# One encoder block: two projections at 512 columns through DRAM, and three joints' loads moved

## The chip, the cores and the metric

The kernel runs on one core of a Trainium2 chip. Its engines each work through a queue of their own in order: TensorE (PE in the profile; PEld is its weight load), VectorE (DVE), ScalarE (ACT), GpSimd (POOL) and SyncE (SP), which here only issues DMAs. The metric is the device time of one execution in microseconds (us), lower is better. Three runs of the kernel before took 1698.77 to 1700.16 us, median 1699.96.

## The reference

One layer of a hybrid encoder on 1024 tokens of 1024 channels, all in float32. Three token mixers share one input projection; then comes a gated feed-forward net.

```python
        h = _rmsnorm(x, norm_mix_g[l])
        z = h @ w_in[l].astype(jnp.float32)
        (hq, hf, hi, hg, fq, fk, fv, ff, mq, gate_logits) = jnp.split(z, pts, axis=-1)
        y_a = _hgrn2_mixer(hq, hf, hi, hg, lower_bounds[l], hgrn_norm_g[l])
        y_b = _fox_mixer(fq, fk, fv, ff, fox_f_bias[l], fox_q_norm_g[l], fox_k_norm_g[l])
...
        y_c = _memory_mixer(mq, mem_kv, mem_q_norm_g[l], mem_k_norm_g[l])
        gates = jax.nn.sigmoid(gate_logits).reshape(B, T, N_BRANCH, D_MODEL)
        merged = (gates[:, :, 0] * (y_a @ w_br_hgrn[l].astype(jnp.float32))
                  + gates[:, :, 1] * (y_b @ w_br_fox[l].astype(jnp.float32))
                  + gates[:, :, 2] * (y_c @ w_br_mem[l].astype(jnp.float32)))
        x = x + (merged @ w_out[l].astype(jnp.float32)).astype(x.dtype)
        h2 = _rmsnorm(x, norm_ffn_g[l])
        x = x + _conv_glu_ffn(h2, ffn_w_up[l], ffn_conv_w[l], ffn_conv_b[l], ffn_w_down[l]).astype(x.dtype)
```

There are 4 recurrence heads with a 128x128 state, 8 attention heads of 64 channels, and 4 heads over 256 memory tokens. The middle mixer is causal softmax attention whose logits carry a cumulated log of forget gates. Its queries and keys (`fq`, `fk`) are normalized per head. The recurrence needs values (`hi`), queries, a forget gate and an output gate.

## The kernel before

**Products.** Each float32 product is three matmuls: operands are split into a rounded part (`h`) and the rest (`l`), and `mm3` (L160 to L162) forms h·h, h·l and l·h. A `split` (L172) is a cast on ScalarE (L166) and a subtraction on VectorE (L174). Weights come by DMA into `raw` (two buffers), and their parts lie in `wh` and `wl` with three buffers each of 128x1056.

**Order.** The program is written in Python generators. `weave` (L97) interleaves them by fixed step counts, `ahead` (L148) gives attention a higher priority, `tc.issue_after` ties an instruction behind another, and a list scheduler of the framework then fixes each engine's order when the kernel is built. On the chip each engine follows its order, so an instruction that must wait holds all behind it.

**Stages.** From the start to 205 us: normalized input `u`, first gates, and pairs of 128-column chunks by a Strassen-like scheme. Then `token_major` (L704) forms projections with tokens on the partitions: for 8 blocks of 128 tokens, 8 pieces of channels and three matmuls each, 256 columns wide. It makes the attention's values `Vf` (`fox_values`), then for each pair of heads `p` its 128 key and 128 query columns (`fox_proj`, L844). A block is evicted by ScalarE into `z` (two tiles of four blocks); after four blocks the tile is normalized. `fox_prep` (L866) transposes `z` and makes the operands `kh`, `kl`, `qa`.

**Attention.** `fox_attn` (L901) takes a head in eight blocks of 128 queries, two by two. Per block: logits on TensorE into `lg` (L924, L925), bias, maximum and mask on VectorE (L930), exp on ScalarE (L940), reciprocal on VectorE (L941), scaling on GpSimd (L942). Per two blocks: transposes on TensorE into `tr` (L953 to L956), split by ScalarE and VectorE into `ph`, `pl`, and products with the head's values `vhl` into `po` (L965, L966). `vhl` is split from `Vf` by `fox_vsplit` (L896), has two buffers, and so waits for the last product two heads back. There are two `lg`, two `tr`, one `po` and three `pp` accumulators.

Between the attention's matmuls the kernel weaves others that depend on little: while head 2p runs, the projection for the next two heads; while head 2p+1 runs, three chunks of gates (`gates_early` with `NFOX`, L31). During heads 6 and 7 come the recurrence's values (`hgrn_values`, L1012), in two passes of 256 columns, whose evictions overwrite `Vf`.

**Later joints.** The branch products (`branch`, L1280) take the attention's and the recurrence's outputs, then the memory branch's, `yc`, which POOL loads in eight transfers of 512 KB (L1311). After `w_out`, `first_products` (L1425) starts the feed-forward net's first unit with operands loaded early; `second_norm` (L1413) sums squares by matmuls with `ones`, GpSimd takes the power (L179), and `spread` (L361) copies the result over partitions by matmuls (L366). `unit` (L1452) loads a unit's weights on POOL's queue (L1457). Between units of the first pair `families` splits operand blocks; two of B21's subtractions run on GpSimd.

Of the kernel before, what the change touches and what calls it, by code (L numbers as in the profile page):

```python
# [30 lines left out]
NFOX = [0, 3, 0, 3, 0, 3, 1]  # L31
# [3 lines left out]
assert 2 + NCOVER + NPAIR + sum(NFOX) == len(ORDER) and len(_dense) % 2 == 0  # L35
# [5 lines left out]
FOX_LATE = 0.2  # L41
SEQ = ("w0 x0 s0 w1 x1 s1 w2 x2 s2 w3 x3 s3 w4 x4 s4 x5 s5 x6 s6 x7 s7 u0 u1 u2 u3 mn u4 u5 u6 u7 lk k0 k1 k2 k3 lx "
# [67 lines left out]
def tile_block(ctx: ExitStack, tc: tile.TileContext, xT, memT, x_rows, mem_rows, vec, fbias, mats, hmask, w_first, w_cm, w_hi, w_fqk, w_fv,  # L110
# [77 lines left out]
    def weights(src, shape, raw=None, hl=None, parts=1):  # L188
# [4 lines left out]
        if hl is None:  # L193
            hl = [wp.tile([P, 4 * 264], F32R, tag=t, name=t, bufs=3) for t in ("wh", "wl")]
# [227 lines left out]
    def first_weights(k):  # L422
        k0, k1 = WFIRST[k]
        if k % 4 == 0:
            gw[k // 4] = [wp.tile([P, 4 * 264], F32R, tag=t, name=t, bufs=3) for t in ("wh", "wl")]
        sl = slice((k0 % 4) * 256, (k1 - 1) % 4 * 256 + 256)
        split(S, gw[k // 4][0][:, sl], gw[k // 4][1][:, sl], wg[k // 4][:, sl])
# [131 lines left out]
    class Dense:  # L559
# [16 lines left out]
        def operand(self, src):  # L576
            if self.half is None:
                self.half = [wp.tile([P, 4 * 264], F32R, tag=t, name=t, bufs=3) for t in ("wh", "wl")]
# [125 lines left out]
    def token_major(src, ncol, evac):  # L704

        with tc.issue_after(late["load"].ins):
            w = [weights(src[q], (4, ncol)) for q in range(2)]
        for tb in range(8):
            ps = ps_proj()[:, :ncol]
            tsl = slice(tb * P, (tb + 1) * P)  # L710
            for k in range(KC):
                wh, wl = w[k // 4]
                mm3(ps, uh[k][:, tsl], ul[k][:, tsl], wh[:, k % 4, :], wl[:, k % 4, :], k == 0, k == KC - 1)
# [129 lines left out]

    def fox_proj(p):  # L844

        fox_z[p] = [None, None]

        def evac(tb, ps):
            n, b = tb // 4, tb % 4
            if b == 0:  # L850
                fox_z[p][n] = pq.tile([P, 4, 256], F32, tag="z", name=f"z{p}_{n}", bufs=2)
            z = fox_z[p][n]
            S.activation(z[:, b, :], ps, AF.Copy, scale=rt[:, tb:tb + 1])
            if b == 3:
                zz = z.rearrange("p b (h d) -> p (b h) d", d=64)
                sq = pools["pf"].tile([P, 16, 64], F32, tag="pt", name="fsq", bufs=4) if p else \
                    pm.tile([P, 16, 64], F32, tag="fsq", name="fsq")
                r = cp.tile([P, 16], F32, tag="fr", name="fr", bufs=2)
                S.activation(sq, zz, AF.Square)
                V.reduce_sum(r, sq, axis=AX.X)  # L860
                rstd_small(r, r, 64)
                V.tensor_mul(zz, zz, r.unsqueeze(2).to_broadcast([P, 16, 64]))

        yield from token_major(w_fqk[p], 256, evac)

# [414 lines left out]
    def branch(br, yh, yl, js=range(8)):  # L1280
        for j in js:
            i = order.index((br, j))
            gts = []
            for n in range(2):
                gt = gate_tile()
                SP.dma_start(gt, gd[i, n])
                gts.append(gt)
            for n, ps in br_chunk(br, j, yh, yl):
# [17 lines left out]
    py = Rounded(tc, name="py", bufs=1, side="right", reuse_waits="tile")  # L1306
    yc = [[py.tile([P, T], F32R, tag=f"yc{p}{c}", name=f"yc{p}{c}") for c in range(4)] for p in "hl"]
    for c in range(4):
# [506 lines left out]
```

## Time and profile before

| what | value |
| --- | --- |
| median of three runs | 1699.96 us |
| profiled execution, its own time | 1700.23 us |
| its span | 1698.4 us |
| instructions | 24291 |
| HBM read, written | 180.72 MB, 67.93 MB |
| attention (first to last logits) | 326.7 to some 654 us |

The profile is one execution. "Busy" is the time in which an engine had an instruction at work, and its share is of the span. A group line gives line, engine, operation, output and inputs, count, then busy time in us and the mean of one in ns, then the engine's idle time just before, with what ended it. A window line gives the stretch, its length, then for PE, PEld, DVE, ACT and POOL the busy us with the number of instructions, the granted clock of TensorE, and the DMA share and GB/s.

### The profile page before, as it was taken

How to read it: one execution, taken by the hardware profiler on the slowest of the kernel's cores; microseconds unless marked ns; L12 is line 12 of the kernel's file. 1: busy time of each engine (PE TensorE's matmuls, PEld its weight loads, DVE VectorE, ACT ScalarE, POOL GpSimd, SP SyncE). 2: the span in 40 equal slices, each digit the busy share in tenths (PEclk: the TensorE clock that was granted, in tenths of full speed). 3: DMA queues.
4: the chain of work that ended last, by engine and by line, in shares of the span. 5: the costliest groups of instructions: out<-in, count | busy, mean ns of one | idle time of the engine just before them, and what ended most of it. 6: DMA issues, size and time to landing. Idle time of an engine off the chain costs nothing.

```text
span 1698.4 us, 24291 instructions
## 1 busy us (share of the span) xinstructions
PE 1691.0 (100%) x8957; PEld 1452.4 (86%) x8957; DVE 1150.8 (68%) x2057; ACT 800.9 (47%) x1428; POOL 324.6 (19%) x420
## 2 busy tenths in 40 slices
PE   9999999999999999999999999999999999999999
PEld 7888899989898998888888888888888888888887
DVE  6966455666666664886856845987878888775654
ACT  6734455545454553775631333644434444533432
POOL 0200032543433331544310000311111111100000
PEclk9999999999999999999999999999999999999999
DMA  9443232221212111110346542566544344494772
GB/s 367 157 161 106 88 139 68 77 92 51 94 59 77 63 46 57 67 32 13 106 127 209 167 186 100 165 174 169 158 139 138 118 149 143 172 363 145 251 269 87
DMA packets 83062, 227.16 MB, mean 134 GB/s; under 512 B 9712, under 2 KB 12408, under 8 KB 82816
## 3 DMA queue, kind: packets, MB, share of 16 engines
q1 hardware_dynamic: 64320, 160.54, 26.8%
q0 software_dynamic: 18048, 64.50, 13.2%
q8 instruction: 70, 1.15, 0.3%
q10 hardware_dynamic: 576, 0.59, 0.1%
q14 instruction: 48, 0.39, 0.1%
HBM read 180.72 MB, written 67.93 MB: 146 GB/s over the span
## 4 chain that ended last, share of the span: by engine, by line
PE 99%; DVE 0%; ACT 0%; DMA 0%; issue 0%; ACTq 0%; DVEq 0%
PE pp L160 21%; PE pp L162 21%; PE pp L161 21%; PE lg L160 4%; PE lg L162 4%; PE lg L161 4%; PE tr L162 3%; PE tr L161 3%; PE tr L160 3%; PE po L966 1%; PE lg L925 1%; PE lg L924 1%; PE po L965 1%; PE po L160 1%; PE po L161 1%; PE po L162 1%
## 5 line engine op out<-in xcount | busy, mean ns | idle before, releaser
L160 PE MATMUL pp<-uh,wh 128*128 128x512 f32 x412 | 163.3, 396 | 0.0
L161 PE MATMUL pp<-ul,wh 128*128 128x512 f32 x412 | 162.9, 395 | 0.0
L162 PE MATMUL pp<-uh,wl 128*128 128x512 f32 x412 | 162.5, 394 | 0.0
L161 PE MATMUL pp<-wl,uh 128*128 128x256 f32 (+1 forms) x512 | 146.3, 286 | 0.0
L162 PE MATMUL pp<-wh,ul 128*128 128x256 f32 (+1 forms) x512 | 146.1, 286 | 0.0
L160 PE MATMUL pp<-wh,uh 128*128 128x256 f32 (+1 forms) x512 | 145.6, 286 | 0.0
L166 ACT CAST wh<-s 128x512 fp32r<-128x512 f32 x110 | 66.5, 621 | 131.6 <-PE pp L161 55.1
L166 ACT CAST wh<-raw 128x1024 fp32r<-128x1024 f32 (+2 forms) x76 | 67.6, 890 | 100.6 <-PE pp L161 86.2
L166 ACT CAST wh<-rw 128x512 fp32r<-128x512 f32 x87 | 53.2, 619 | 108.1 <-PE pp L161 70.2
L160 PEld LDWEIGHTS pp<-wh,uh 128*128 128x128 f32 x512 | 97.3, 190 | 1.2
L161 PEld LDWEIGHTS pp<-wl,uh 128*128 128x128 f32 x512 | 97.4, 190 | 1.0
L162 PEld LDWEIGHTS pp<-wh,ul 128*128 128x128 f32 x512 | 97.4, 190 | 0.9
L1457 POOL DMA_DIRECT2D rw<-in_w_up x44 | 24.1, 555 | 372.4 <-DVE wl L1350 171.3
L166 ACT CAST dwh<-wr 128x1024 fp32r<-128x1024 f32 (+1 forms) x41 | 40.2, 980 | 115.8 <-PE tr L161 40.0
L162 PEld LDWEIGHTS pp<-uh,wl 128*128 128x128 f32 x412 | 77.5, 188 | 15.1
L174 DVE TENSOR_TENSOR wl<-raw,wh 128x1024 fp32r<-128x1024 f32 (+2 forms) x75 | 78.0, 1040 | 17.8 <-ACT wh L166 17.6
L160 PEld LDWEIGHTS pp<-uh,wh 128*128 128x128 f32 x412 | 77.5, 188 | 14.6
L161 PEld LDWEIGHTS pp<-ul,wh 128*128 128x128 f32 x412 | 77.5, 188 | 14.5
L940 ACT ACTIVATE pt<-pt,st 128x128 f32<-128x128 f32 (+3 forms) x64 | 49.7, 777 | 41.7 <-DVE st L937 33.9
L174 DVE TENSOR_TENSOR dwl<-wr,dwh 128x1024 fp32r<-128x1024 f32 (+1 forms) x41 | 46.3, 1129 | 31.7 <-ACT dwh L166 31.7
L942 POOL TENSOR_SCALAR pt<-pt,st 128x128 f32<-128x128 f32 (+3 forms) x64 | 49.1, 767 | 78.4 <-DVE st L941 64.1
L1350 DVE TENSOR_TENSOR wl<-rw,wh 128x512 fp32r<-128x512 f32 x69 | 47.7, 704 | 22.7 <-PE pp L162 18.2
(500 smaller groups left out, 5123.2 us busy)
## 6 DMA issues: line engine op xcount, KB each, us to landing
rw<-in_w_up POOLq DMA_DIRECT2D x44, 512.0 KB, 4.7
sd<-in_w_dn POOLq DMA_DIRECT2D x30, 512.0 KB, 6.0
br<-yd SPq DMA_DIRECT2D x30, 512.0 KB, 5.0
raw<-in_w_cm SPq DMA_DIRECT2D x24, 512.0 KB, 3.4
gd<-gt SPq DMA_DIRECT2D x48, 256.0 KB, 2.0
gt<-gd SPq DMA_DIRECT2D x48, 256.0 KB, 2.7
yd<-fc SPq DMA_DIRECT2D x44, 256.0 KB, 2.2
wr<-sd SPq DMA_DIRECT2D x20, 512.0 KB, 4.5
```

The source lines that it names most:

```text
L160: PE.matmul(ps, lh, rh, start=first, stop=False, skip_group_check=more)
L161: PE.matmul(ps, lh, rl, start=False, stop=False, skip_group_check=more)
L162: return PE.matmul(ps, ll, rh, start=False, stop=last, skip_group_check=more)
L166: return S.copy(out, in_)
L174: return (sub or V).tensor_sub(l, src, h.bitcast(F32))
L924: PE.matmul(ps[:, :w], qa[i][:, tsl], kh[i][:, s0:s0 + w], start=True, stop=False)
L925: fox_sets[p][3] = PE.matmul(ps[:, :w], qa[i][:, tsl], kl[i][:, s0:s0 + w], start=False, stop=True)
L940: S.activation(pt[:, :ns], pt[:, :ns], AF.Exp, bias=st[:, 2:3], accum_out=st[:, 3:4])
L942: G.tensor_scalar(pt[:, :ns], pt[:, :ns], st[:, 3:4], 0.0, ALU.mult, ALU.add)
L965: PE.matmul(o, vhl[:, sb, :], ph[:, src], start=(sb == 0), stop=False)
L1350: late["split"] = V.tensor_sub(l, src, h.bitcast(F32))
L1457: late["raw"] = G.dma_start(raw[:, 2 * i:2 * i + 2, :], src[:, 2 * i:2 * i + 2, :])
```

## The change

It has four parts.

1. The key and query columns of heads 4 to 7 are projected together, 512 columns at once, and so are the recurrence's 512 value columns; weights come in four pieces of two channel blocks. `wh` and `wl` get a fourth buffer, and the scratch for DMA descriptors is cut to 4096. The projection of heads 4 to 7 goes block by block to DRAM (`zd`), and `fox_load` brings two `z` tiles back per pair of heads, a head earlier than they were formed before.
2. The gates that cover the attention are dealt out anew: three, two, three and one chunks beside heads 3, 4, 5 and 6, one beside head 1.
3. The memory branch's loads are spread over the steps of the branch before it, by marks on GpSimd.
4. The second feed-forward unit's load is tied behind GpSimd's B21 subtraction.

```diff
-NFOX = [0, 3, 0, 3, 0, 3, 1]
+NFOX = 10
...
+WIDE = 4
...
-            hl = [wp.tile([P, 4 * 264], F32R, tag=t, name=t, bufs=3) for t in ("wh", "wl")]
+            hl = [wp.tile([P, 4 * 264], F32R, tag=t, name=t, bufs=WIDE) for t in ("wh", "wl")]
...
-            w = [weights(src[q], (4, ncol)) for q in range(2)]
+            per = 2 if ncol == HB else 4
+            w = [weights(src[q], (per, ncol)) for q in range(KC // per)]
...
+    def fox_proj_late():
+
+        def evac(tb, ps):
+            t = gate_tile()
+            S.activation(t, ps, AF.Copy, scale=rt[:, tb:tb + 1])
+            SP.dma_start(zd[tb], t)
+
+        yield from token_major(w_late[0], HB, evac)
+
+    def fox_load(p):
+        cs = slice((p - 2) * 256, (p - 1) * 256)
+        for n in range(2):
+            z = fox_tile(p, n)
+            SP.dma_start(z, zd[4 * n:4 * n + 4, :, cs].rearrange("b p c -> p b c"))
+            fox_norm(p, z)
+            yield
...
+    late_proj = fox_proj_late()
+    first = (fox_proj(1), chain(islice(late_proj, 4), fox_load(2)), gates_early(2))
+    second = (chain(gates_early(1), islice(late_proj, 4)), gates_early(3), gates_early(3))
     for p in range(3):
-        weave((ahead(fox_attn(p, 0), AHEAD), FOX_STEPS), (fox_proj(p + 1), 8))
+        weave((ahead(fox_attn(p, 0), AHEAD), FOX_STEPS), (first[p], (8, 6, 4)[p]))
         fox_prep(p + 1, fox_sets[p][3])
-        weave((ahead(fox_attn(p, 1), AHEAD), FOX_STEPS), (gates_early(NFOX[2 * p + 1]), 2 * NFOX[2 * p + 1], FOX_LATE))
+        weave((ahead(fox_attn(p, 1), AHEAD), FOX_STEPS), (second[p], 6, FOX_LATE),
+              *([(fox_load(3), 2, 0.1)] if p == 1 else []))
+    run_all(late_proj)
...
-        for pc in range(2):
-            def evac(tb, ps, pc=pc):
-                S.activation(Vf[:, tb, pc * 256:(pc + 1) * 256], ps, AF.Copy, scale=rt[:, tb:tb + 1])
-            yield from token_major(w_hi[pc], 256, evac)
+        def evac(tb, ps):
+            S.activation(Vf[:, tb, :], ps, AF.Copy, scale=rt[:, tb:tb + 1])
+        yield from token_major(w_late[1], HB, evac)
...
-        weave((ahead(fox_attn(3, i), AHEAD), FOX_STEPS), (islice(values, 8), 8),
-              (gates_early(0 if i else NFOX[6]), 2 * NFOX[6], FOX_LATE))
+        weave((ahead(fox_attn(3, i), AHEAD), FOX_STEPS), (chain(gates_early(1 - i), islice(values, 4)), 6 - 2 * i))
...
-    for c in range(4):
-        for t, d in zip(yc, ycd):
-            with tc.issue_after(state["norm"].ins):
-                G.dma_start(t[c], d[:, c, :].bitcast(F32R))
-    run_all(branch(0, yh, yl))
+    for i, _ in enumerate(first_branch):
+        if i % 3 and i < 12:
+            p, c = i % 3 - 1, i // 3
+            mark = G.tensor_scalar(warm, late["gates"][:, 0:1], 1.0, 0.0, ALU.mult, ALU.add)
+            with tc.issue_after(mark.ins):
+                G.dma_start(yc[p][c], ycd[p][:, c, :].bitcast(F32R))
...
-            late["raw"] = G.dma_start(raw[:, 2 * i:2 * i + 2, :], src[:, 2 * i:2 * i + 2, :])
+            with tc.issue_after(late["pool"].ins) if after else nullcontext():
+                late["raw"] = G.dma_start(raw[:, 2 * i:2 * i + 2, :], src[:, 2 * i:2 * i + 2, :])
...
-    nc = bacc.Bacc("TRN2", target_bir_lowering=False, num_devices=1)
+    nc = bacc.Bacc("TRN2", target_bir_lowering=False, num_devices=1, dynamic_dma_scratch_size=4096)
```

What each engine then works through follows from the scheduler. The first place is TensorE's order during head 5 (names: `kh1_2`, `qa1_2` are that head's operands, `kh0_3` head 6's; `pp` with `uh`, `ul` is a projection or a gate). In the kernel before, after the logits of head 5's fifth block:

```order
L924 MATMUL lg_5935<-kh1_2_4722,qa1_2_4724 128x512
L925 MATMUL lg_5935<-kl1_2_4726,qa1_2_4724 128x512
L161 MATMUL pp_6403<-ul1_82,wh_6399 128x512
L965 MATMUL po_5602<-ph_5672,vhl_5235 128x256
L162 MATMUL pp_6403<-uh1_81,wl_6400 128x512
L160 MATMUL pp_6403<-uh2_83,wh_6399 128x512
L161 MATMUL pp_6403<-ul2_84,wh_6399 128x512
L162 MATMUL pp_6403<-uh2_83,wl_6400 128x512
L160 MATMUL pp_6403<-uh3_85,wh_6399 128x512
L966 MATMUL po_5602<-pl_5673,vhl_5235 128x256
L965 MATMUL po_5602<-ph_5672,vhl_5235 128x128
```

There a gate's matmuls stand between the attention's, and so it is all through the head. In the changed kernel the last matmuls of a block of values, after which head 5's third logits begin the stretch that the prediction speaks of:

```order
L161 MATMUL pp_6456<-wh_6276,uh7_93 128x512
L162 MATMUL pp_6456<-wl_6277,uh7_93 128x512
L163 MATMUL pp_6456<-wh_6276,ul7_94 128x512
L950 MATMUL lg_5657<-kh1_2_4625,qa1_2_4627 128x384
L951 MATMUL lg_5657<-kl1_2_4629,qa1_2_4627 128x384
L980 MATMUL tr_5472<-ident_72,pt_5453 128x128
L979 MATMUL tr_5472<-ident_72,pt_5435 128x128
L980 MATMUL tr_5472<-ident_72,pt_5453 128x128
L991 MATMUL po_5357<-ph_5388,vhl_5156 128x256
```

From there on every row is the attention's, up to head 6's seventh logits, behind which the next block of values stands:

```order
L991 MATMUL po_6138<-ph_6143,vhl_6070 128x256
L992 MATMUL po_6138<-pl_6144,vhl_6070 128x256
L991 MATMUL po_6138<-ph_6143,vhl_6070 128x128
L992 MATMUL po_6138<-pl_6144,vhl_6070 128x128
L950 MATMUL lg_6397<-kh0_3_5556,qa0_3_5558 128x512
L951 MATMUL lg_6397<-kl0_3_5560,qa0_3_5558 128x512
L950 MATMUL lg_6401<-kh0_3_5556,qa0_3_5558 128x384
L951 MATMUL lg_6401<-kl0_3_5560,qa0_3_5558 128x384
L161 MATMUL pp_6511<-wh_6258,uh0_79 128x512
L162 MATMUL pp_6511<-wl_6259,uh0_79 128x512
```

So the matmuls of gates and values that stood inside this stretch now stand before and behind it.

The second place is POOL's queue at the joint into the feed-forward net (`rw` is a unit's weights, `rw_10864` and `rw_11001` the first and second unit's; `rt2` the second norm's power; `B21l` the subtractions; `sd` sums of weights in DRAM). Before:

```order
L1457 DMA rw_10864<-in_w_up 128x1024 x2
L1457 DMA rw_11001<-in_w_up 128x1024 x2
L179 TENSOR_TENSOR rt2_10790<-rt2_10790,mhalf_75 128x8
L1522 DMA sd_10863<-in_w_dn 128x1024
L174 TENSOR_TENSOR B21l0_10859<-x1_6_10194,B21h0_10858 128x512
L174 TENSOR_TENSOR B21l0_10859<-x1_7_10195,B21h0_10858 128x512
L1457 DMA rw_11153<-in_w_up 128x1024 x2
```

And now (`rw_10477` and `rw_10614` are the first and second unit's):

```order
L180 TENSOR_TENSOR rt2_10403<-rt2_10403,mhalf_75 128x8
L1490 DMA rw_10477<-in_w_up 128x1024 x2
L175 TENSOR_TENSOR B21l0_10472<-x1_6_9807,B21h0_10471 128x512
L175 TENSOR_TENSOR B21l0_10472<-x1_7_9808,B21h0_10471 128x512
L1490 DMA rw_10614<-in_w_up 128x1024 x2
L1556 DMA sd_10476<-in_w_dn 128x1024
```

The first unit's load moved behind the power, the second unit's behind both subtractions.

The third place is TensorE at the same joint, around the matmuls that spread `rt2`. Before, they stand behind the product T3:

```order
L160 MATMUL pp_10791<-T3h0_10856,wh2_10869 128x512
L161 MATMUL pp_10791<-T3l0_10857,wh2_10869 128x512
L162 MATMUL pp_10791<-T3h0_10856,wl2_10870 128x512
L366 MATMUL tr_10897<-ident_72,rt2_10790 128x128 x4
L366 MATMUL tr_10903<-ident_72,rt2_10790 128x128 x4
L160 MATMUL pp_11020<-B11h0_10175,wh2_11004 128x512
L161 MATMUL pp_11020<-B11l0_10176,wh2_11004 128x512
```

And now one matmul into the product B22, which is ahead of T3:

```order
L162 MATMUL pp_10404<-T2l0_9793,wh_10369 128x512
L163 MATMUL pp_10404<-T2h0_9792,wl2_10380 128x512
L161 MATMUL lg_10405<-B22h0_10467,wh2_10384 128x512
L367 MATMUL tr_10510<-ident_72,rt2_10403 128x128 x4
L367 MATMUL tr_10516<-ident_72,rt2_10403 128x128 x4
L162 MATMUL lg_10405<-B22l0_10468,wh2_10384 128x512
L163 MATMUL lg_10405<-B22h0_10467,wl2_10385 128x512
```

They moved up by 23 matmuls.

More of the change, by code (lines that the diff above doesn't have):

```diff
@@ L577, in operand @@
             if self.half is None:
-                self.half = [wp.tile([P, 4 * 264], F32R, tag=t, name=t, bufs=3) for t in ("wh", "wl")]
+                self.half = [wp.tile([P, 4 * 264], F32R, tag=t, name=t, bufs=WIDE) for t in ("wh", "wl")]
                 h, l = (t[:, :HB] for t in self.half)
@@ L1287, in branch @@
                 gts.append(gt)
+            late["gates"] = gts[0]
             for n, ps in br_chunk(br, j, yh, yl):
@@ L1360, in first_operands @@
         a11, a21, a22, a12 = raw
-        h = [wp.tile([P, 4 * 264], F32R, tag="wh", name="wh", bufs=3) for _ in range(2)]
-        sums = [wp.tile([P, 4 * 264], F32R, tag="wl", name="sums", bufs=3).bitcast(F32) for _ in range(2)]
+        h = [wp.tile([P, 4 * 264], F32R, tag="wh", name="wh", bufs=WIDE) for _ in range(2)]
+        sums = [wp.tile([P, 4 * 264], F32R, tag="wl", name="sums", bufs=WIDE).bitcast(F32) for _ in range(2)]
         s1, s2, s4 = sums[0][:, :HB], sums[0][:, HB:2 * HB], sums[1][:, :HB]
@@ L1504, in families @@
                 for k in range(4):
-                    late["last"] = family_block(name, k, quarters(k)[q], G if name == "B21" and k > 1 else None)
+                    sub = G if name == "B21" and k > 1 else None
+                    late["pool" if sub else "last"] = family_block(name, k, quarters(k)[q], sub)
             if name == "T3":
@@ L1776, in pieces @@
         return out
-    o["w_hi"] = c(np.stack(pieces(hi, [(0, 256), (256, 512)])))
     o["w_fqk"] = c(np.stack([pieces(np.concatenate([fk[:, p * P:(p + 1) * P], fq[:, p * P:(p + 1) * P]], axis=1),
-                                    [(0, 256)])[0] for p in range(4)]))
+                                    [(0, 256)])[0] for p in range(2)]))
+    late = np.concatenate([m[:, p * P:(p + 1) * P] for p in (2, 3) for m in (fk, fq)], axis=1)
+    o["w_late"] = c(np.stack([kmaj(m).reshape(P, 4, 2 * HB).transpose(1, 0, 2) for m in (late, hi)]))
     pv = pieces(np.concatenate([fv, ff], axis=1), [(0, 256), (256, 520)])
```

38 lines of the change are left out of this document (22 added, 16 removed).

## Prediction

> **What bounds the kernel now.** I read the page's first and fourth parts, then the view of who waited for whom, kept to TensorE.
>
> ```profile
> span 1698.4 us, 24291 instructions
> PE 1691.0 (100%) x8957; PEld 1452.4 (86%) x8957; DVE 1150.8 (68%) x2057; ACT 800.9 (47%) x1428; POOL 324.6 (19%) x420
> PE 99%; DVE 0%; ACT 0%; DMA 0%; issue 0%; ACTq 0%; DVEq 0%
> PE lg L160 <- ACT uh L349: 1.8, 1, 1.8
> PE tr L265 <- POOL dull L263: 1.0, 1, 1.0
> PE po L1189 <- DVE St L1195: 0.7, 1, 0.7
> PE pp L162 <- DVE wl L1350: 0.2, 1, 0.2
> ```
>
> TensorE (PE) is the chain, and its waits are four, 3.7 us in all. So time is won only by fewer or cheaper matmuls, and any new wait of TensorE is lost in full. The profiled execution took 1700.23 us, 1.8 beside its span; the median of the runs is 1699.96, so sums against 1700.2 hold for both.
>
> A matmul's own duration misleads, since matmuls overlap. The timeline of TensorE gives start to start (columns: start, us, engine, line, operation): first and last of 20 records 256 wide, then of 19 records 512 wide.
>
> ```profile
> 210.66 0.28 PE L160 MATMUL pp<-wh,uh 128*128 128x256 f32 x1
> ...
> 212.93 0.28 PE L160 MATMUL pp<-wh,uh 128*128 128x256 f32 x1
> 904.79 0.39 PE L162 MATMUL pp<-yh,wl 128*128 128x512 f32 x1
> ...
> 908.87 0.39 PE L162 MATMUL pp<-yh,wl 128*128 128x512 f32 x1
> ```
>
> 2.27 us over 19 steps is 0.1195 us for 256 columns; 4.08 over 18 is 0.2267 for 512.
>
> **Part 1, the wide projections.** Four products of 256 columns go (keys and queries of heads 4 and 5, of 6 and 7, and both halves of the values): 4 x 8 token blocks x 8 x 3 = 768 matmuls, 91.8 us. Two of 512 columns come: 384 matmuls, 87.0 us. **-4.7 us.** Weight casts, subtractions and loads stay eight of 128x1024; evictions halve from 32 to 16, on engines that don't bound.
>
> [...]
>
> The way over DRAM (eight stores of 256 KB, four loads of 512 KB) I cost at nothing. In TensorE's new order some 390 places, about 70 us at the intervals above, stand between the last matmul of that projection and the first transpose of what is reloaded for heads 4 and 5. If that cover were gone, a store (2.0) and a load (3.7) with the norm behind them would cost some 12 us.
>
> ```profile
> gd<-gt SPq DMA_DIRECT2D x48, 256.0 KB, 2.0
> nf<-negFd SPq DMA_DIRECT2D x8, 512.0 KB, 3.7
> ```
>
> The fourth weight buffer frees slots earlier almost everywhere, where nothing waited anyway: 0, at most 1 us either way. The spread loads of the memory branch still end about 14 us of matmuls ahead of their first reader: 0.
>
> **Part 2, the cover that leaves heads 5 and 6.** Take the stretch from head 5's third logits to head 6's seventh. Before, the same stretch stands here in the trace (its first logits at 548.93, its last from 616.34), and this is the view of busy time by window for it (PE, PEld, DVE, ACT, POOL), then for head 0, for the 42 us around it, and for the quickest of the seven stretches of this kind (head 6's third logits to head 7's seventh):
>
> ```profile
> 548.93 0.34 PE L924 MATMUL lg<-kh,qa 128*128 128x384 f32 x1
> 616.34 0.34 PE L924 MATMUL lg<-kh,qa 128*128 128x384 f32 x1
> 548.90:616.30 67.40, 67.40 (x506) 64.27 (x505) 43.06 (x131) 37.31 (x75) 25.32 (x37) 1.00 0.18 58
> 326.70:353.50 26.80, 26.80 (x193) 25.10 (x191) 20.87 (x70) 17.02 (x34) 14.91 (x20) 1.00 0.21 63
> 320.00:362.00 42.00, 42.00 (x295) 39.12 (x294) 29.68 (x84) 24.25 (x47) 23.64 (x28) 1.00 0.21 68
> 597.90:649.80 51.90, 51.90 (x389) 49.54 (x388) 33.08 (x114) 28.54 (x62) 16.23 (x26) 1.00 0.20 61
> ```
>
> 67.4 us, and TensorE never idle: 280 matmuls of 256 and 50 of 512 columns (44.8 us) stood between the attention's own, which leaves 22.6 us for attention. In the new order there is none of these 330: the gates run ahead, three blocks of values fill the three accumulators, and their eviction overwrites Vf, which the split for head 7 must have read first; that split waits for head 5's last product. TensorE, in order, then has 22.6 us of attention and must wait for the other engines. VectorE (DVE) has 100 instructions between those logits. These are the costliest forms in the grouped view of the window, with mean ns:
>
> ```profile
> L174 DVE TENSOR_TENSOR pl<-tr,ph 128x512 fp32r<-128x512 f32 x10 | 6.8, 683 | 2.5 <-ACT ph L166 2.5
> L930 DVE CUSTOM_DVE_ANT_0 pt<-lg,nf 128x512 f32<-128x512 f32 x7 | 4.8, 688 | 5.6 <-PE tr L953 2.9 <-PE lg L925 2.5
> L174 DVE TENSOR_TENSOR pl<-tr,ph 128x384 fp32r<-128x384 f32 x7 | 3.9, 553 | 0.3 <-ACT ph L166 0.2
> L890 DVE SCALAR_TENSOR_TENSOR qa<-tr,fqs,qa 64x512 fp32r<-64x512 f32 x4 | 3.0, 750 | 2.3 <-ACT qa L889 2.2
> L884 DVE SCALAR_TENSOR_TENSOR kl<-tr,cv,kh 64x512 fp32r<-64x512 f32 x4 | 3.0, 750 | 2.9 <-ACT kh L883 2.9
> 604.47 0.21 DVE L937 TENSOR_SCALAR st<-st 128x1 f32<-128x1 f32 x1
> 604.59 0.68 DVE L174 TENSOR_TENSOR pl<-tr,ph 128x512 fp32r<-128x512 f32 x1
> ```
>
> Seven, six, six, four and four of these are 19 us; with the other 73 at their means it is 31.8 us without the 25 read-outs, which overlap whole. The last two rows show the next instruction starting about 0.08 us before the end of the one ahead: 75 x 0.075 off leaves **26.2 us**, the floor: at least 3.6 us of waiting. VectorE doesn't run without holes here, as each softmax passes four engines in turn: its share is 0.78 in head 0 and 0.71 in the 42 us around it. I take 0.71, the longer row, since no other work fills its holes now: 36.9 us, **+14.3 us**. The upper end is the quickest such stretch, 51.9 us with other matmuls among it: +29.3.
>
> **Part 3, the joint into the ConvGLU.** Two loads on POOL's queue move: the first unit's behind the second norm's power, the second unit's behind two subtractions. Rows of before: the product that begins the joint (T0 = 1062.10), POOL's loads, power and subtractions, the norm's 16 records and a load's time from issue to landing.
>
> ```profile
> 1062.10 0.39 PE L160 MATMUL pp<-B11h,wh 128*128 128x512 f32 x1
> 1053.27 1.06 POOL L1457 DMA_DIRECT2D rw<-in_w_up  x2 [163.03 <-ACT sqs L1392]
> 1068.02 1.05 POOL L1457 DMA_DIRECT2D rw<-in_w_up  x2 [13.69 <-ACT B22h L166]
> 1071.70 2.65 POOL L179 TENSOR_TENSOR rt<-rt,mhalf 128x8 f32<-128x8 f32 x1 [2.63 <-DVE rt L178]
> 1075.13 2.98 POOL L174 TENSOR_TENSOR B21l<-x,B21h 128x512 fp32r<-128x512 f32 x2 [0.23 <-ACT B21h L166]
> L1416 PE MATMUL po<-ones,r x16: 165/250/251, 1067.5 to 1070.5; 128*128 128x1 f32 x16
> rw<-in_w_up POOLq DMA_DIRECT2D x44, 512.0 KB, 4.7
> 1072.13 0.69 DVE L1449 TENSOR_TENSOR s<-rw 128x512 f32<-128x512 f32 x1
> 1072.85 0.62 ACT L166 CAST wh<-s 128x512 fp32r<-128x512 f32 x1
> ```
>
> The norm's sums end at T0+8.7, the power (2.65) at T0+11.5. The matmuls that spread it now stand at T0+10.0 on TensorE, before T3: 1.5 us of waiting. The first unit's load starts at T0+11.5 where it started at T0-8.8; with 4.7, 0.69 and 0.62 its operand is there at T0+17.5, and T3, due at T0+14.9, waits 2.6. Then ScalarE casts three B21 parts, two operands and the fourth part (some 3.3 us, T0+20.8), POOL's last subtraction (1.5) ends at T0+22.3, the second unit's load lands at T0+27.0, and its operand is cast at T0+27.6. TensorE comes there 24 matmuls after T3's start, T0+22.9, and waits 4.7. Together 8.8; the 0.2 that it waits here now goes: **+8.5 us**, from nothing (if the operands came from elsewhere) to 10. Behind these waits on POOL stand only DRAM sums that nobody waits for yet.
>
> **Sum.** 1700.2 - 4.7 + 14.3 + 8.5 = 1718.3: **1718 us**.
>
> **Rivals.**
> The first, on the other side: the attention keeps up and the joint's loads are early enough. That is decided by whether VectorE needs more than TensorE's 22.6 us in the stretch. For it speaks that TensorE has had no wait in any attention; against it that this attention always had 2 us of other matmuls for each one of its own. It gives 1700.2 - 4.7 = 1695.5.
> The second: only one of the two is real, the stretch at its floor (3.6) with half of the joint, 1703.4, or the joint hidden, 1709.8.
> The third: TensorE slows down once it idles. It would run the stretch's 22.6 us at half speed, 45 us between waits, +22 for +14 and 1726. The window rows show a clock of 1.00, but in a TensorE that never idled, so they neither bear it out nor exclude it. [...]
>
> **How the numbers follow.** Forecast (both waits near their sizes) 0.76; second rival 0.10; third 0.07; first 0.07. The range takes the floor of the stretch with five for the joint, 1704, up to the stretch near its upper end, 1732; the third rival lies inside. A measurement tells 0.2% (3.4 us) from no change. Faster by more: the first, 0.07; within: the lowest of the second, 0.05; slower: the rest, 0.88.
>
> **What would show it.** Right: between head 5's third and head 6's seventh logits the window shows VectorE over 0.65 and TensorE with some 14 us idle, put down to VectorE or ScalarE; T3 and the second unit's first product wait some 7 us for the cast of a load; start to start at 512 columns stays 0.227. Wrong: TensorE without waits there, or waits at weight casts or at the reload from DRAM.

## The result and the profile after

The changed kernel takes 1718.49 us, the median of four runs (1716.83 to 1718.94), beside 1700.06 (1698.77 to 1700.18) for the kernel before on the same chip: a ratio of 1.0108, interval 1.0091 to 1.0126. The profiled execution took 1718.15 us, 1.8 more than its span. These are the page's span, busy times and chain by engine:

```profile
span 1716.4 us, 23549 instructions
PE 1695.0 (99%) x8573; PEld 1432.6 (83%) x8573; DVE 1150.4 (67%) x2057; ACT 795.8 (46%) x1412; POOL 329.5 (19%) x428
PE 86%; issue 9%; DVE 2%; DMA 1%; ACT 1%; POOL 0%; ACTq 0%; POOLq 0%; DVEq 0%; SPq 0%
```

TensorE issues 384 matmuls fewer, as the change says, and still the span is 18 us longer. Its share hides this: 99% of a longer span. The chain shows it, for it no longer runs through TensorE alone. The view of who waited for whom, TensorE only (total us, times, longest), then names the new waits:

```profile
PE tr L904 <- issue: 3.3, 1, 3.3
PE tr L979 <- DVE kl L910: 2.4, 1, 2.4
PE tr L162 <- DVE B21l L175: 1.8, 1, 1.8
PE pp L161 <- ACT wh L167: 1.7, 2, 0.9
PE tr L367 <- POOL rt L180: 0.7, 1, 0.7
```

The first two lie in the attention, the other three at the joint into the feed-forward net. By start to start on TensorE the kernel divides so (from first to last matmul it is 17.7 us longer):

| part | before | after | change | predicted |
| --- | --- | --- | --- | --- |
| projections of 512 columns (not measured alone: what the other rows leave of 17.7) | | | -4.6 | -4.7 |
| head 5's third to head 6's seventh logits | 22.6 of attention (beside 44.8 of others) | 38.1 | +15.5 | +14.3 |
| joint, from its first product (B11) into the third product T4 behind it | 65.2 (from 1062.1) | 72.0 (from 1072.9) | +6.8 | +8.5 |
| down projection to the end | 203.8 | 203.8 | 0 | 0 |

Between the attention and the joint TensorE waits only 0.7 us, at the recurrence's `St`, as before: no wait for the memory branch's spread loads shows.

**The stretch.** Its first logits start at 574.27, its last at 612.33. This is the window between (PE, PEld, DVE, ACT, POOL busy, then the clock), and two parts of it:

```profile
574.30:612.40 38.10, 29.09 (x175) 22.77 (x173) 31.58 (x116) 25.73 (x55) 19.71 (x34) 0.91 0.09 26
586.50:593.40 6.90, 4.47 (x20) 3.64 (x19) 5.96 (x15) 4.33 (x9) 2.91 (x5) 0.51 0.01 4
593.40:612.40 19.00, 16.62 (x101) 12.55 (x99) 16.46 (x74) 13.31 (x31) 9.90 (x17) 1.00 0.14 43
```

TensorE is without a record for 38.10 - 29.09 = 9.0 us; VectorE works 31.58, a share of 0.83. In the second window TensorE runs at half its clock (0.51). The two long waits on the timeline, and VectorE beside them:

```profile
581.81 0.27 PE L951 MATMUL lg<-kl,qa 128*128 128x128 f32 x1
585.35 0.63 PE L904 MATMUL tr<-ident,z 128*128 128x128 f32 x4 [3.27 <-issue]
586.18 0.74 PE L904 MATMUL tr<-ident,z 128*128 128x128 f32 x4 [0.21 <-DVE qa L916]
589.36 0.45 PE L979 MATMUL tr<-ident,pt 128*128 128x128 f32 x1 [2.43 <-DVE kl L910]
584.49 0.76 DVE L910 SCALAR_TENSOR_TENSOR kl<-tr,cv,kh 64x512 fp32r<-64x512 f32 x1
585.28 0.76 DVE L916 SCALAR_TENSOR_TENSOR qa<-tr,fqs,qa 64x512 fp32r<-64x512 f32 x1
586.73 0.74 DVE L910 SCALAR_TENSOR_TENSOR kl<-tr,cv,kh 64x512 fp32r<-64x512 f32 x1 [0.69 <-ACT kh L909]
587.68 0.74 DVE L916 SCALAR_TENSOR_TENSOR qa<-tr,fqs,qa 64x512 fp32r<-64x512 f32 x1 [0.20 <-ACT qa L915]
588.45 0.76 DVE L910 SCALAR_TENSOR_TENSOR kl<-tr,cv,kh 64x512 fp32r<-64x512 f32 x1
```

"Issue" at the first wait doesn't mean that nothing was waited for: the transposes start at 585.35, 0.1 us after the `kl` at 584.49 has ended, which reads one of the two `tr` buffers. So both waits are for conversions of heads 6 and 7's keys and queries, which VectorE takes one after the other, almost without a gap. They hold `tr`, and the next matmul in TensorE's order needs it. The way over DRAM is not what is waited for: VectorE has normalized the last `z` tile by 528.6.

These two waits are not all of it. From the logits at 581.81 to the transposes at 589.36 TensorE starts nine records in 7.6 us; at the mean steps of the same forms in the kernel before they would take 0.9 (an estimate). Counted in that way, 1.8 us are lost ahead of this part, 6.7 in it, 2.1 in the rest of the half clock and 6.3 behind 593.4, where no wait is over 0.63. (That is 17.0, since by these steps the attention needs 21.5 and not 22.6.) The third row of the window is this last part: no conversion of keys or queries stands in it, only softmax and products, and VectorE is busy 0.87 of it.

**The joint.** POOL and VectorE on the timeline (T0, its first product, is 1072.94), then TensorE's waits:

```profile
1081.92 2.03 POOL L180 TENSOR_TENSOR rt<-rt,mhalf 128x8 f32<-128x8 f32 x1 [149.15 <-DVE rt L179]
1083.92 1.12 POOL L1490 DMA_DIRECT2D rw<-in_w_up  x2
1093.95 1.10 POOL L1490 DMA_DIRECT2D rw<-in_w_up  x2
1081.66 0.17 DVE L179 TENSOR_SCALAR rt<-po 128x8 f32<-128x8 f32 x1 [3.49 <-PE po L1448]
1081.74 2.49 DVE L175 TENSOR_TENSOR B22l<-x,B22h 128x512 fp32r<-128x512 f32 x4
1091.48 3.07 DVE L1382 TENSOR_TENSOR wl<-rw,wh 128x512 fp32r<-128x512 f32 x2 [0.96 <-ACT wh L167]
1094.47 1.28 DVE L175 TENSOR_TENSOR B21l<-x,B21h 128x512 fp32r<-128x512 f32 x2
1084.01 2.05 PE L367 MATMUL tr<-ident,rt 128*128 128x128 f32 x16 [0.68 <-POOL rt L180]
1089.42 0.50 PE L161 MATMUL pp<-T3h,wh 128*128 128x512 f32 x1 [0.82 <-ACT wh L167]
1095.21 0.50 PE L162 MATMUL tr<-B21l,wh 128*128 128x512 f32 x1 [1.80 <-DVE B21l L175]
1098.89 0.50 PE L161 MATMUL pp<-B11h,wh 128*128 128x512 f32 x1 [0.88 <-ACT wh L167]
```

There are four waits: for the power, for T3's operand, for VectorE's part of B21, which stands behind the weights' 3.07 us, and for the second unit's operand. None is long; start to start, with three smaller ones, they make 6.2 of the 6.8.

### The profile page after: what moved, and what is told of

Its sections match the earlier page's. It is cut to its first block, busy times and chain, and to the rows that moved or that the text cites. A ratio compares the mean times of both kernels' runs of the same rounds, so it can differ in the third digit from the quotient of the medians.

```text
span 1716.4 us, 23549 instructions
## 1 busy us (share of the span) xinstructions
PE 1695.0 (99%) x8573; PEld 1432.6 (83%) x8573; DVE 1150.4 (67%) x2057; ACT 795.8 (46%) x1412; POOL 329.5 (19%) x428
## 4 chain that ended last, share of the span: by engine, by line
PE 86%; issue 9%; DVE 2%; DMA 1%; ACT 1%; POOL 0%; ACTq 0%; POOLq 0%; DVEq 0%; SPq 0%
PE pp L161 18%; PE pp L162 18%; PE pp L163 18%; PE lg L161 4%; PE lg L163 4%; PE lg L162 4%; PE tr L161 3%; PE tr L162 3%; PE tr L163 3%; PE po L992 1%; PE po L161 1%; PE po L163 1%; PE po L162 1%; PE po L991 1%; PE lg L1184 1%
## 5 line engine op out<-in xcount | busy, mean ns | idle before, releaser
L162 PE MATMUL pp<-wl,uh 128*128 128x256 f32 (+2 forms) x384 | 123.8, 323 | 0.0
L161 PE MATMUL pp<-wh,uh 128*128 128x256 f32 (+2 forms) x384 | 123.3, 322 | 0.0
L163 PE MATMUL pp<-wh,ul 128*128 128x256 f32 (+2 forms) x384 | 123.2, 321 | 0.0
L167 ACT CAST wh<-raw 128x1024 fp32r<-128x1024 f32 (+2 forms) x76 | 67.7, 892 | 96.6 <-PE pp L162 86.0
L162 PEld LDWEIGHTS pp<-wl,uh 128*128 128x128 f32 x384 | 72.8, 190 | 5.1
L163 PEld LDWEIGHTS pp<-wh,ul 128*128 128x128 f32 x384 | 72.8, 190 | 5.0
L161 PEld LDWEIGHTS pp<-wh,uh 128*128 128x128 f32 x384 | 72.8, 189 | 4.8
L956 DVE CUSTOM_DVE_ANT_0 pt<-lg,nf 128x512 f32<-128x512 f32 (+3 forms) x80 | 41.5, 524 | 35.9 <-PE lg L951 19.3
L1382 DVE TENSOR_TENSOR wl<-rw,wh 128x512 fp32r<-128x512 f32 x69 | 48.1, 712 | 22.9 <-PE pp L163 18.5
L167 ACT CAST ph<-tr 128x512 fp32r<-128x512 f32 (+1 forms) x80 | 41.3, 543 | 47.3 <-PE po L991 19.2
```

Of the source, the lines that this page charges most:

```text
L161: PE.matmul(ps, lh, rh, start=first, stop=False, skip_group_check=more)
L162: PE.matmul(ps, lh, rl, start=False, stop=False, skip_group_check=more)
L163: return PE.matmul(ps, ll, rh, start=False, stop=last, skip_group_check=more)
L167: return S.copy(out, in_)
L956: V.tensor_tensor_reduce(out=pt[:, s0 + lo:s0 + hi], in0=ps[:, lo:hi], in1=bias, op0=ALU.add, op1=ALU.max, scale=1.0, scalar=-3e38, accum_ ...
L1382: late["split"] = V.tensor_sub(l, src, h.bitcast(F32))
```

## The experiments

The theory after the comparison: both losses are waits behind other engines, the first because no matmul without a dependence stands in the stretch, the second because loads and power come late. Rivals: the lower clock in the stretch, rather than the wait, makes it long; the way over DRAM costs something; and, at the joint, the order that the scheduler chose rather than the hold of the load. Each of these kernels was timed in five rounds beside the kernel before.

**Cover tied back (c1_cover), joint undone (c2_joint), both (c3_cover_joint).** In c1, each gate and each late projection is tied to the logits issued last:

```diff
+                with tc.issue_after(late["logits"].ins) if tie else nullcontext():
+                    mm3(ps, uh[k][:, tsl], ul[k][:, tsl], wh[:, k % per, :], wl[:, k % per, :], k == 0, k == KC - 1)
...
```

In c2 the hold is gone, and the power is issued behind B22's subtractions instead:

```diff
-        rstd_small(rt2, ps[:, :8], D)
+        late["norm sums"] = ps
...
-            with tc.issue_after(late["pool"].ins) if after else nullcontext():
-                late["raw"] = G.dma_start(raw[:, 2 * i:2 * i + 2, :], src[:, 2 * i:2 * i + 2, :])
+            late["raw"] = G.dma_start(raw[:, 2 * i:2 * i + 2, :], src[:, 2 * i:2 * i + 2, :])
...
+            if name == "B22":
+                with tc.issue_after(late["last"].ins):
+                    rstd_small(rt2, late["norm sums"][:, :8], D)
```

> The changed kernel with the same dense matmuls, but each gate of heads 1 to 6 and each block of the wide projection of keys and queries held until the logits issued just ahead of it in the program, so that they stand between the attention's own matmuls in every head and heads 5 and 6 have 18 to 24 of them at every second logits again. Theory A (the 15.5 us that the stretch lost are the missing cover): the stretch from head 5's third to head 6's seventh logits has no wait of TensorE over 0.6 us, its clock reads 1.00, and the kernel takes 1703 to 1706 us, 13 to 15.5 under the changed one. Theory B (the loss comes with the wide projection itself: the way over DRAM, or the longer hold of weight buffers): waits of 5 us or more stay in heads 2 to 6 and the kernel takes 1710 or more.

> The changed kernel with the joint into the ConvGLU in the old order: the hold of the second unit's load is taken out, and the second norm's VectorE step stands behind the low parts of B22, which puts both units' loads ahead of the norm's power on POOL and the spread behind T3's first matmuls. Theory A (the joint's 6.7 us are the two loads and the norm's place): from the first product to the end of the first unit TensorE loses under 1.5 us and the kernel takes 1711 to 1713. Theory B (the joint waits for something else, as the spread loads of the memory branch or the operands' buffers): 1716 or more.

> Both edits, the cover of c1_cover and the joint of c2_joint. Theory A: the two losses are all that stands against the narrower count of matmuls, so the kernel takes 1695 to 1698 us, 2 to 5 under the kernel before. Theory B (the saving of 4.7 us by wide products is not real, or the waits move elsewhere): 1700 or more.

c1 took 1730.96 us, 1.0186 [1.0171, 1.0201]: slower still, so the expected gain failed, and by its time alone it would fall under theory B (1710 or more). Its largest waits of TensorE, in the same view:

```profile
PE tr L906 <- DVE qa L918: 3.7, 1, 3.7
PE lg L952 <- DVE st L958: 3.6, 4, 2.2
PE tr L981 <- DVE kl L912: 3.3, 3, 2.9
PE tr L981 <- DVE pl L175: 2.9, 3, 2.1
```

The waits moved to heads 1, 3 and 5, again behind the conversions after each set of `z` transposes and behind the softmax. Matmuls tied in lumps of 24 to one pair of logits leave bare places between the lumps, and some 100 of them now ran only behind head 7. So the cover was not restored, and the run decides nothing between the theories.

c2 took 1713.81, 1.0084 [1.0069, 1.0099], 4.7 below the changed kernel, and the joint lasts 67.7 us, 2.5 above before; the expectation (1711 to 1713, under 1.5 us lost) was too low. Its POOL and VectorE have the old order again: load, then power; B22 ahead of the norm.

```profile
1081.92 1.05 POOL L1489 DMA_DIRECT2D rw<-in_w_up  x2 [28.88 <-PE pp L163]
1083.97 1.87 POOL L180 TENSOR_TENSOR rt<-rt,mhalf 128x8 f32<-128x8 f32 x1
1078.47 2.50 DVE L175 TENSOR_TENSOR B22l<-x,B22h 128x512 fp32r<-128x512 f32 x4 [1.54 <-ACT B22h L167]
1080.88 0.16 DVE L179 TENSOR_SCALAR rt<-po 128x8 f32<-128x8 f32 x1
```

So this order, with the hold gone, is worth 4.4 of the joint's 6.8. The load shown is the second unit's, which still starts late (T0+10.2, for T0+5.9 before), and three waits of 0.6, 0.6 and 0.7 us for the weights' parts are left. c3 took 1728.30, 1.0168 [1.0153, 1.0183], 2.7 below c1, and its number failed as c1's did. Its joint is 4.5 us shorter than c1's (c2's 4.4 shorter than the changed kernel's), so this loss is separate from the stretch; ahead of the joint c3 takes 2.9 us more than c1, for which no run shows the cause.

**More cover for the stretch (c5_supply).** Three pairs of gate chunks are not formed by the Strassen-like scheme at the start but one by one beside heads 5 and 6. Nothing is tied:

```diff
-NCOVER, NPAIR = 2, 10
+NCOVER, NPAIR = 2, 4
...
-NFOX = 10
+NFOX = 16
...
-    second = (chain(gates_early(1), islice(late_proj, 4)), gates_early(3), gates_early(3))
+    second = (chain(gates_early(1), islice(late_proj, 4)), gates_early(3), gates_early(7))
...
-        weave((ahead(fox_attn(3, i), AHEAD), FOX_STEPS), (chain(gates_early(1 - i), islice(values, 4)), 6 - 2 * i))
+        weave((ahead(fox_attn(3, i), AHEAD), FOX_STEPS), (chain(gates_early(3 * (1 - i)), islice(values, 4)), 6 - 2 * i))
```

> The changed kernel with three of the five pairs of gates that are multiplied by seven products in the first stage turned back into six plain gates that are woven into the attention (84 matmuls of 512 columns a pair become 96, so 36 more, +8.2 us at 0.227). Nothing is tied to a place: the planner has 288 more dense matmuls to put between the attention's own. Theory A (the 15.5 us are missing cover, and c1_cover failed because blocks of 24 tied to single logits left other places bare): TensorE has no wait over 0.6 us in the eight heads, its clock reads 1.00 there, and the kernel takes 1718.3 + 8.2 - 15.5 = 1711 us, between 1709 and 1713. Theory B (the attention loses time here for another reason, as the way over DRAM or the weight buffers): the waits stay and it takes 1722 or more.

Measured: 1711.96, 1.0072 [1.0058, 1.0086], where 1711 was expected. Head 5's third to head 6's seventh logits now stand at 518.6 and 601.8; this is that window, then the two largest rows of TensorE's waits in the whole kernel:

```profile
518.60:601.80 83.20, 83.20 (x441) 70.85 (x440) 46.44 (x132) 38.22 (x72) 21.18 (x34) 1.00 0.23 76
PE pp L161 <- ACT wh L167: 1.9, 2, 1.2
PE lg L161 <- ACT uh L350: 1.6, 1, 1.6
```

TensorE is busy through all 83.2 us, at a clock of 1.00, and neither of these waits lies in the attention. The bill closes: -4.7 for the projections, +8.2 for three pairs undone (each is 12 matmuls of 0.2267 us more), +7.2 for this kernel's joint, together 10.7 beside 11.4 measured between first and last matmul; 0.7 is not assigned. So the 15.5 us were missing cover, and the way over DRAM costs nothing that shows.

**Is it the clock (c4_fill, c9_fill_both)?** One pair of logits is repeated, as added work: in c4 twelve times ahead of the first long wait, in c9 eight times there and eight in the second. c4:

```diff
+                    for _ in range(12 if (h, tb, s0) == (5, 4, HB) else 0):
+                        PE.matmul(ps[:, :w], qa[i][:, tsl], kh[i][:, s0:s0 + w], start=True, stop=False)
+                        PE.matmul(ps[:, :w], qa[i][:, tsl], kl[i][:, s0:s0 + w], start=False, stop=True)
```

c9 has eight for twelve, and behind the pair the same once more, tied to the last `z` transposes:

```diff
+                    for _ in range(8 if (h, tb, s0) == (5, 4, HB) else 0):
+                        with tc.issue_after(late["z"].ins):
+                            PE.matmul(ps[:, :w], qa[i][:, tsl], kh[i][:, s0:s0 + w], start=True, stop=False)
...
```

> The changed kernel with 24 more matmuls of 128 columns, which repeat one logits product of head 5 (its result is unchanged by the repeats) just ahead of the 3.27 us that TensorE waits at the transposes of the last pair's keys and queries; nothing else in TensorE's order changes there. Theory A (TensorE's clock fell for 8 us because of that wait, and the slow matmuls cost 2 to 2.5 us): the clock reads 1.00 through the stretch and the stretch is 1.5 to 2.5 us shorter, 1716 to 1717. Theory B (the slow matmuls only used up time that TensorE would have waited for VectorE): the stretch stays within 0.5 us of 38.1, and the kernel at 1718 to 1719.

> The changed kernel with two groups of 16 matmuls of 128 columns that repeat one logits product of head 5 (its result is unchanged by the repeats), one group ahead of the 3.27 us wait at the transposes of the last pair's keys and queries and one in the 2.43 us wait behind them; c4_fill had filled the first alone, and the half clock then came 4 us later all the same, behind the second wait. A few attention instructions change places about 10 us later. Theory A (the half clock costs time of its own, about 2 us, since TensorE is busy without a hole in its last 3.9 us): the clock reads 1.00 all through, and the stretch from head 5's third to head 6's seventh logits is 36 to 36.7 us instead of 38.1. Theory B (what TensorE loses there it would wait for VectorE anyway): 37.6 us or more.

c4 took 1719.14, 1.0120 [1.0103, 1.0136]; the stretch lasts 37.9 us for 38.1 in the changed kernel, as theory B has it. The first wait fell from 3.27 to 0.6, and its transposes came no earlier. The clock in two windows of c4:

```profile
586.00:590.00 4.00, 1.36 (x10) 0.73 (x8) 3.15 (x5) 2.73 (x4) 3.10 (x6) 1.00 0.00 0
590.00:594.00 4.00, 3.73 (x17) 3.54 (x17) 3.76 (x17) 2.40 (x6) 1.08 (x3) 0.57 0.01 2
```

Half clock lasted 3.4 us here (590.5 to 593.9) where the changed kernel has 6.8 (586.6 to 593.4; the 8 of the expectation were too many), and no time was won: in the half that went, TensorE mostly waited. c9 should have taken the other half away too, and failed: 1719.68, 1.0116 [1.0101, 1.0132], stretch 39.4 us. Its clock fell all the same, behind a wait of only 1.48 us, and the repeats in the second wait ran at half speed (0.21 us apart from 585.74 on, for 0.11 between 580.3 and 582). So the lower clock alone was not removed; what it costs the changed kernel stays open, bounded by half of the 4.0 us in which TensorE runs at it without a hole (589.4 to 593.4, busy 4.00 at a clock of 0.50), an estimate: at most 2 us of 15.5.

**The joint's parts (c6_fourth_buffer, c7_no_hold).** c6 is the kernel before with the fourth weight buffer and the smaller scratch, c7 the changed kernel without the hold:

```diff
-            hl = [wp.tile([P, 4 * 264], F32R, tag=t, name=t, bufs=3) for t in ("wh", "wl")]
+            hl = [wp.tile([P, 4 * 264], F32R, tag=t, name=t, bufs=4) for t in ("wh", "wl")]
...
-    nc = bacc.Bacc("TRN2", target_bir_lowering=False, num_devices=1)
+    nc = bacc.Bacc("TRN2", target_bir_lowering=False, num_devices=1, dynamic_dma_scratch_size=4096)
```

```diff
-            with tc.issue_after(late["pool"].ins) if after else nullcontext():
-                late["raw"] = G.dma_start(raw[:, 2 * i:2 * i + 2, :], src[:, 2 * i:2 * i + 2, :])
+            late["raw"] = G.dma_start(raw[:, 2 * i:2 * i + 2, :], src[:, 2 * i:2 * i + 2, :])
```

> The kernel before with nothing but the fourth weight buffer (and the smaller DMA scratch that makes room for it). In the planner's order this alone puts the second norm's VectorE step ahead of B22's low parts, both units' loads behind the norm's power on POOL, and the spread into B22. Theory A (this order, not the hold, is the larger part of the joint's 6.7 us): TensorE waits some 3 to 5 us between the joint's first product and the end of the first unit, and the kernel takes 1702 to 1705 us. Theory B (the hold of the second unit's load is what costs): 1699 to 1701.

> The changed kernel with only the hold of the second unit's load taken out, so that this load follows the first unit's directly, both still behind the norm's power. Theory A (the hold costs only the wait at the second unit's first product): that wait of 1.05 us goes, and with it perhaps the wait of 1.97 at B21's low part, 1715 to 1717.5. Theory B (the hold is most of the joint's loss): 1713 or less.

c6 took 1706.77, 1.0039 [1.0027, 1.0052], above the range expected. From the first attention logits up to the joint its timeline runs 0.4 us ahead of before, throughout; in the joint it loses 6.6, and after it nothing. Its POOL, VectorE and waits:

```profile
1070.69 2.04 POOL L179 TENSOR_TENSOR rt<-rt,mhalf 128x8 f32<-128x8 f32 x1 [180.83 <-DVE rt L178]
1072.69 2.16 POOL L1457 DMA_DIRECT2D rw<-in_w_up  x4
1070.43 0.17 DVE L178 TENSOR_SCALAR rt<-po 128x8 f32<-128x8 f32 x1 [3.49 <-PE po L1416]
1070.52 2.49 DVE L174 TENSOR_TENSOR B22l<-x,B22h 128x512 fp32r<-128x512 f32 x4
PE tr L161 <- DVE B21l L174: 2.4, 1, 2.4
```

The power ahead of the loads, B22 behind the norm: the order of the changed kernel without the hold, with no other part of the change present. What costs time is this order: the scheduler, which plans with the buffer, puts four rows otherwise. The smaller scratch was not changed alone, and no run has the wide projections with three buffers. Not all of the 6.6 need be the order's: behind the wait of 2.4 the first matmul with B21's low part took 0.80 us (from 1084.69), where the changed kernel's took 0.50 (from 1095.21). c7 has that order too: it took 1716.86, 1.0100 [1.0086, 1.0114], as theory A expected, with a joint of 70.9 us, 5.7 above before. So the hold costs 1.1 of the 6.8 (1.6 by the medians, whose intervals overlap; the joints of the changed kernel, c1, c4 and c9, where it is the same, lie within 0.2). The wait for the second unit's operand is gone there, and the one at B21 grew from 1.8 to 2.4.

**Is there a better mixture (c8_mixed, c10_two_pairs)?** c8 is c2 with one pair undone, and the values in two products of 256 columns again; c10 is c2 with two pairs undone:

```diff
-        yield from token_major(w_late[1], HB, evac)
+        for pc in range(2):
+            def evac(tb, ps, pc=pc):
+                S.activation(Vf[:, tb, pc * 256:(pc + 1) * 256], ps, AF.Copy, scale=rt[:, tb:tb + 1])
+            yield from token_major(w_hi[pc], 256, evac)
...
```

```diff
-NCOVER, NPAIR = 2, 10
+NCOVER, NPAIR = 2, 6
...
-NFOX = 10
+NFOX = 14
...
-    second = (chain(gates_early(1), islice(late_proj, 4)), gates_early(3), gates_early(3))
+    second = (chain(gates_early(1), islice(late_proj, 4)), gates_early(3), gates_early(5))
...
```

> The changed kernel with the joint of c2_joint, with the recurrence's values as two products of 256 columns again (+2.4 us: 384 matmuls at 0.1195 for 192 at 0.2267; the first half writes only columns that heads 0 to 3 have read, so it may run under heads 4 to 6), and one pair of gates turned back into two plain ones (+2.7). The wide projection of keys and queries stays. Theory A: no wait over 0.6 us in the attention, 1713.8 - 15.5 + 2.4 + 2.7 = 1703 us, 1701 to 1706, so still not under the kernel before. Theory B (the way of keys and queries over DRAM costs by itself): waits at the transposes of the reloaded tiles, 1710 or more.

> The joint of c2_joint, and two of the five pairs turned back into four plain gates (c5_supply had three): +5.4 us of matmuls, and 192 more dense matmuls to put between the attention's. In the planner's order head 5 is covered to its end, the conversions for heads 6 and 7 with it, and head 6 is bare up to its sixth row of blocks. Theory A (what is lost goes with the length of the bare stretch, and the conversions were the costly part of it): 3 to 7 us of waits, none over 1.5, in head 6, the clock at 1.00; 1713.8 + 5.4 - 15.5 + 5 = 1709 us, 1706 to 1711. Theory B (a shorter bare stretch costs as much as the long one): 1714 or more.

c8 took 1711.64, 1.0069 [1.0056, 1.0082], far from 1703, but not as theory B has it, with waits at the reloaded tiles. Its attention has no wait, but the start of the recurrence has (685 to 708 us):

```profile
PE tr L1205 <- DVE kE L1197: 2.6, 1, 2.6
PE pp L161 <- DVE gt L1077: 2.2, 1, 2.2
PE lg L1133 <- DVE X L1129: 1.2, 1, 1.2
```

What covered the next stage had been spent on this one: between head 7's last logits and the joint 508 matmuls with `uh` or `ul` are left, where c2 has 533. c10 took 1707.90, 1.0044 [1.0032, 1.0057], inside the range expected (1706 to 1711): 1700.2, -4.7, +5.4 for two pairs and +2.5 for the joint make 1703.4, and five waits of 0.3 to 0.6 (start to start) in head 6 some 2.5 more; 2 us are not assigned. It is the best version of the change found, and it doesn't beat the kernel before: cover costs 2.7 us a pair, and two pairs are more than the wide projections bring.

## Why the prediction was right

**Projections, -4.7:** in keeping with the runs, though none has this part alone: the other rows leave -4.6, TensorE has 384 matmuls fewer, and their interval is as before. First and last of ten records of the values on TensorE's timeline of the changed kernel, 2.04 us over nine steps, are 0.2267 apart:

```profile
639.83 0.39 PE L162 MATMUL pp<-wl,uh 128*128 128x512 f32 x1
...
641.87 0.39 PE L162 MATMUL pp<-wl,uh 128*128 128x512 f32 x1
```

The way over DRAM at nothing: confirmed by c5, where no wait for it appears. The view of DMAs has eight stores and four loads with medians of 2.0 and 3.4 us.

**The stretch, +14.3:** measured +15.5, and c5 shows the mechanism. That TensorE must wait here for VectorE was right; that the size came so near is luck, for both factors were off and the errors cancel. I took 26.2 us of VectorE work at a share of 0.71; the window has 31.58 at 0.83. The measured work at my share would be 44.5 us, my work at the measured share 31.6; the stretch took 38.1. Sixteen more VectorE instructions fell between these logits than I counted. (And the five forms that I summed to 19 us make 18.2.)

The share failed for a reason that carries over. I read 0.78 and 0.71 in windows where TensorE was busy all the time (26.80 of 26.80, 42.00 of 42.00), so VectorE there followed TensorE, and its holes were not the softmax's own. Without the other matmuls it is busy 0.87 where softmax and products stand alone (593.4 to 612.4), and about as much, 6.99 of 8.10, around the conversions (581.9 to 590.0). So the passing through four engines does not hold VectorE at 0.71.

The 14 us of idle time that I named are 9.0 without a record. Of the rest of the 15.5 at most 2 are half clock; that the others are short waits and ends of single matmuls, which overlap in a stream, is my reading and not measured apart.

**The joint, +8.5:** (its terms, 8.8 less 0.2, make 8.6.) Measured +6.8, near in the sum and again partly by luck, since terms that were too large stand beside a wait that was not forecast. The two waits for the cast of a load, some 7 us in my signs, are 1.7. The spread waits 0.7 for the 1.5 I gave it, T3's first operand 0.8 and its low part 0.4 for 2.6: POOL's power took 2.03 us where the row of before has 2.65, so the load starts at T0+11.0 and not T0+11.5, and the operand is cast at T0+16.4 and not T0+17.5, while T3 is due at T0+15.5 and not T0+14.9. The second unit waits 0.9 (1.0 start to start) for 4.7. TensorE was due there at T0+24.9 instead of T0+22.9, since it had waited 1.8 for VectorE's B21, which the prediction did not have and which is the joint's longest wait; and the operand was there at T0+25.9 instead of T0+27.6, POOL being done earlier. Two errors of attribution remain. I gave the fourth buffer "0, at most 1 us either way": with it and the smaller scratch alone c6 loses 6.6 in the joint; by c7 the order is worth 5.7. And the hold of the second load, which I charged most, is the smaller part: without it c7 still loses 5.7.

**Rivals.** Nothing waits (1695.5): excluded. Only one real: excluded, as c5 takes the stretch's loss away and leaves the joint's, and c2 takes most of the joint's and leaves the stretch's (37.9 us). TensorE slower once it idles (1726): the clock did fall to half, which I gave 0.07, but for 6.8 us and not the whole stretch, and its price is 2 us at most instead of 8. That rival's half speed was an assumption, with no row of before behind it; the changed kernel's trace then showed a clock of 0.50 from 586.56 to 593.39.

## What to carry to other kernels

Fewer or wider matmuls on a busy TensorE won only what the other engines could follow (4.7 us by the count, against 15.5 lost in the stretch): first ask which matmuls without a dependence stand between the attention's, and whether a change moves them. A conversion from a shared accumulator behind a set of transposes needed such cover most (the two longest waits, 3.27 and 2.43 us, stood there), and in c1 dealing it out in lumps only moved the hole. A busy share that was read while another engine set the pace does not say what the engine reaches when it sets the pace itself: 0.71 became 0.87 here. With a list scheduler, one more buffer is a change of order everywhere: compare the orders at each joint before costing it at nothing.

## What the hardware showed

TensorE's clock fell to half for 6.83 us in the changed kernel (586.56 to 593.39, clock 0.50) and in c9 (585.50 to 592.33, 0.50), and for 3.41 us in c4 (590.51 to 593.92, 0.50). The time ahead of a fall was not empty. These are the 3.41 us ahead of it in the changed kernel, in c4 and in c9, in this order, one fence each; TensorE's busy time is the number behind the length:

```profile
583.15:586.56 3.41, 1.00 (x8) 0.83 (x8) 2.75 (x6) 2.44 (x4) 3.09 (x5) 1.00 0.08 19
```

```profile
587.10:590.51 3.41, 0.73 (x5) 0.55 (x6) 3.23 (x5) 2.44 (x4) 2.41 (x4) 1.00 0.00 0
```

```profile
582.09:585.50 3.41, 1.73 (x15) 1.41 (x15) 2.65 (x4) 2.32 (x4) 2.87 (x6) 1.00 0.08 19
```

TensorE was busy for 29%, 21% and 51% of them. The 3.41 us ahead of that in the changed kernel, with 2.10 busy (62%), kept a clock of 1.00, as did those behind them:

```profile
579.74:583.15 3.41, 2.10 (x17) 1.96 (x17) 2.49 (x9) 2.62 (x7) 2.27 (x4) 1.00 0.00 0
```

But the busy share of such a stretch alone does not decide. These 3.41 us of the changed kernel, at the joint, are busy for 49%, and the clock reads 1.00 in them and in the 3.41 us that follow (1095.14 to 1098.55):

```profile
1091.73:1095.14 3.41, 1.68 (x8) 1.03 (x6) 3.41 (x4) 2.84 (x6) 3.15 (x5) 1.00 0.00 0
```

What decides near half stays open. While the clock was at half, TensorE was busy for 4.40 of 6.83 us in the changed kernel, for all 3.41 in c4 and for all 6.83 in c9; what ended it is open too.
